# Sum of reciprocals over rows of 1024: another list of loads and operations for the last 24 rows

## Chip, cores and metric

One core of a Trainium2 chip. The metric is the device time of one execution in microseconds (us). An execution has a span, from its first to its last recorded instruction, which lies some 2 us under the device time. "Row" below is one of the 128 slices of 128 partitions by 1024 columns into which the input is cut, numbered 0 to 127; the last 24 are rows 104 to 127.

## The reference

```python
def reference(x):          # x: 32 x 512 x 1024, float32, positive
    return np.sum(1.0 / x, axis=-1).astype(np.float32)
```

## The kernel before

64 MiB are streamed through a ring of 40 rows in SBUF. A row of 1024 values is taken as two halves a and b of 512, by 1/a + 1/b = (a + b) / (a b). So a row needs the product a b, its Ln, an Exp of minus that (exp(-ln y) is 1/y), and a multiply-and-sum on VectorE, against a + b if TensorE has made that in PSUM (a reduction of 512 columns), or else against the row itself (1024 columns). The last 24 rows are written as a list of steps, and the list alone decides in which order each engine meets them.

```python
LAST = 104
LAST_LOADS = [2] * 10 + [1] * 4              # rows in each load
ORDER = """ P104+ P106 L104+ S109 P107 ... E127 T126 T127 """
# c is the row, "+" takes rows c and c+1 in one instruction
# P  product on GpSimd, both halves from SBUF        -> pr (SBUF)
# D  the same product on VectorE, both from SBUF     -> pr
# B  TensorE copies half b into PSUM; V: product on VectorE, a from SBUF, b from PSUM -> pr
# S  TensorE makes a + b in PSUM
# L  Ln of pr on ScalarE;   E  Exp of minus that
# T  reduction on VectorE: 512 columns where the row has an S, else 1024
# W, X  Ln, then Exp of the whole row (1024) on ScalarE, which also sums it (accum_out)
...
        elif kind == "W":
            keep(nc.scalar.activation(out=rows, in_=rows, func=Ln))
        elif kind == "X":
            keep(nc.scalar.activation(out=rows, in_=rows, func=Exp, scale=-1.0,
                                      accum_out=sums[:, c : c + 1]))
...
nc.sync.dma_start(out=out_v, in_=sums)       # one store, after the last sum
```

## Time and profile before

| | before |
|---|---|
| device time, median of the first 3 runs (range) | 169.75 us (169.62 to 170.16) |
| span of the profiled run | 167.9 us |
| last load complete on all 16 engines | 161.46 us |
| ScalarE's last Exp ends / VectorE's last sum is written | 164.62 / 165.45 us |
| from the last load to the last sum | 3.99 us |
| store issued | 165.47 us |

The last four times come from the trace: the landing marks of the input queue and the ends of the last records. The fifth line tells how much lies behind the stream. The lines that carry this reading stand in the prediction. Columns: start, duration, engine, line, operation, output and input.

### The profile page before, as it was taken

The page shows a single profiled execution, that of the slowest core. Times are in us where ns is not written, and L with a number is a line of the kernel's source. Part 1 is how long each engine was busy: PE and PEld are TensorE (multiplying, and loading weights), DVE is VectorE, ACT ScalarE, POOL GpSimd, SP SyncE. Part 2 cuts the span into 40 slices and gives each one's busy share as a digit, 9 for nine tenths or more (in the row PEclk, how much of TensorE's full clock was granted, in tenths as well). Part 3 has the DMA queues.
Part 4 walks back from the last instruction along what each step waited for, and adds up shares of the span by engine and source line. Part 5 has one row for each costly group of instructions (what it writes and reads, how often), then busy time and mean ns, then how long its engine had stood idle before and what let it go on. Part 6 is the DMA issues. An engine that isn't in the chain of part 4 may idle for free.

```text
span 167.9 us, 1307 instructions
## 1 busy us (share of the span) xinstructions
PE 130.8 (78%) x278; PEld 50.5 (30%) x278; DVE 122.8 (73%) x268; ACT 134.1 (80%) x143; POOL 137.7 (82%) x73
## 2 busy tenths in 40 slices
PE   0007999786989869776797869877999988799991
PEld 0003333232323323222332323333343324243340
DVE  0000677768977677885777787778989898999894
ACT  3001898979888897959879787999999998999992
POOL 1007999699996999859996998999999999979780
PEclk9999999999999999999999999999999999999999
DMA  6999999999999999999999999999999999999900
GB/s 195 429 437 429 445 429 437 437 429 429 406 455 414 445 422 449 422 431 437 429 429 429 429 398 429 427 433 433 420 429 408 423 418 424 422 422 414 382 26 18
DMA packets 4471, 67.25 MB, mean 401 GB/s; under 512 B 496, under 2 KB 624, under 8 KB 1136
## 3 DMA queue, kind: packets, MB, share of 16 engines
q1 hardware_dynamic: 4464, 67.18, 94.4%
q8 instruction: 2, 0.03, 0.1%
q14 instruction: 5, 0.04, 0.1%
HBM read 67.11 MB, written 0.07 MB: 400 GB/s over the span
## 4 chain that ended last, share of the span: by engine, by line
DMA 71%; ACT 11%; POOL 10%; DVE 3%; issue 2%; PE 2%; DVEq 0%; SPq 0%; POOLq 0%; ACTq 0%
DMA ring<-in_x_dram 71%; POOL pr L159 8%; ACT pr L231 5%; ACT pr L237 3%; ACT r L237 2%; POOL pr L213 1%; DVE pr L110 1%; PE s L100 1%; DVE ring L110 1%; ACT pr L170 1%; ACT r L175 1%; PE bb L100 1%; DVE pr L222 0%; DVE sums L110 0%; DVEq L287 0%
## 5 line engine op out<-in xcount | busy, mean ns | idle before, releaser
L100 PE MATMUL s<-ring,ident 128*128 128x512 f32 x256 | 121.4, 613 | 32.2 <-DMA ring<-in_x_dram 16.2
L159 POOL TENSOR_TENSOR pr<-ring 128x1024 f32<-128x1024 f32 (+1 forms) x52 | 112.7, 2202 | 21.5 <-DMA ring<-in_x_dram 21.5
L100 PEld LDWEIGHTS s<-ring,ident 128*128 128x128 f32 x256 | 46.9, 193 | 104.1 <-issue 63.3
L170 ACT ACTIVATE pr<-pr 128x1024 f32<-128x1024 f32 x52 | 54.8, 1053 | 26.9 <-POOL pr L159 26.9
L110 DVE CUSTOM_DVE_ANT_1 pr<-ring,r 128x1024 f32<-128x1024 f32 x27 | 33.0, 1221 | 41.4 <-ACT r L175 41.4
L110 DVE CUSTOM_DVE_ANT_1 ring<-ring,r 128x1024 f32<-128x1024 f32 x37 | 44.8, 1217 | 0.2 <-issue 0.2
L110 DVE CUSTOM_DVE_ANT_0 pr<-pr,s 128x512 f32<-128x512 f32 x64 | 41.5, 683 | 0.3 <-ACT pr L237 0.3
L180 ACT ACTIVATE pr<-pr 128x1024 f32<-128x1024 f32 x26 | 27.5, 1057 | 0.8
L175 ACT ACTIVATE r<-pr 128x1024 f32<-128x1024 f32 x26 | 26.7, 1028 | 0.8
L213 POOL TENSOR_TENSOR pr<-ring 128x512 f32<-128x512 f32 (+1 forms) x15 | 24.5, 1648 | 3.0 <-DMA ring<-in_x_dram 2.4
L231 ACT ACTIVATE pr<-pr 128x512 f32<-128x512 f32 (+1 forms) x17 | 13.0, 794 | 1.0 <-DVE pr L222 0.7
L110 DVE DVE_READ_ACCUMULATOR2_ANT sums<- 128x1 f32 x128 | 10.6, 83 | 0.0
L100 PE MATMUL b<-ring,ident 128*128 128x512 f32 x16 | 8.7, 625 | 0.1
L237 ACT ACTIVATE pr<-pr 128x512 f32<-128x512 f32 (+1 forms) x10 | 6.9, 704 | 0.1
L237 ACT ACTIVATE r<-pr 128x512 f32<-128x512 f32 (+1 forms) x11 | 6.8, 625 | 0.1
L148 DVE TENSOR_TENSOR pr<-ring,b 128x512 f32<-128x512 f32 x8 | 5.5, 682 | 0.0
L100 PEld LDWEIGHTS b<-ring,ident 128*128 128x128 f32 x16 | 2.6, 188 | 5.6 <-DMA ring<-in_x_dram 4.1
L100 PE MATMUL bb<-ring,ident 128*128 128x512 f32 x6 | 3.2, 622 | 1.3 <-DMA ring<-in_x_dram 1.2
L222 DVE TENSOR_TENSOR pr<-ring,bb 128x512 f32<-128x512 f32 x3 | 2.1, 686 | 0.7 <-PE bb L100 0.6
L100 PEld LDWEIGHTS bb<-ring,ident 128*128 128x128 f32 x6 | 1.0, 188 | 3.4 <-DVE sums L110 2.0
L71 ACT ACT_TABLE_LOAD x1 | 1.3, 1283 | 0.7 <-PEq L276 0.7
L215 DVE TENSOR_TENSOR pr<-ring 128x512 f32<-128x512 f32 x1 | 0.9, 864 | 0.0
(6 smaller groups left out, 0.9 us busy)
## 6 DMA issues: line engine op xcount, KB each, us to landing
ring<-in_x_dram SPq DMA_DIRECT2D x10, 4096.0 KB, 37.8
ring<-in_x_dram SPq DMA_DIRECT2D x6, 2048.0 KB, 37.0
ring<-in_x_dram SPq DMA_DIRECT2D x10, 1024.0 KB, 26.0
ring<-in_x_dram SPq DMA_DIRECT2D x4, 512.0 KB, 16.8
out_dram<-sums SPq DMA_DIRECT2D x1, 64.0 KB, 1.5
```

Source lines behind the costliest of these rows:

```text
L71: nc.scalar.add_instruction(mybir.InstLoadActFuncSet(name=nc.get_next_instruction_name(), act_func_set_id=act_sets.index("natural_log_exp_ ...
L100: i = nc.tensor.matmul(bank, lhsT=ident, rhs=half, start=k == 0, stop=k == len(halves) - 1,)
L110: i = nc.vector.tensor_tensor_reduce(out=row if out is None else out, in0=row, in1=fac, scale=S, scalar=0.0, op0=mult, op1=plus, accum_out ...
L148: i = nc.vector.tensor_tensor(out=pr[:, j, :], in0=xt[:, q + j, :H], in1=b, op=mult)
L159: i = nc.gpsimd.tensor_tensor(out=pr[:, v:, :], in0=xc[:, v:, :H], in1=xc[:, v:, H:], op=mult)
L170: keep(nc.scalar.activation(out=pr, in_=pr, func=Ln, scale=S))
L175: nc.scalar.activation(out=r, in_=pr[:, e:, :], func=Exp, scale=-1.0)
L180: keep(nc.scalar.activation(out=r, in_=r, func=Exp, scale=-1.0))
L213: keep(nc.gpsimd.tensor_tensor(out=pr, in0=a, in1=b, op=mult))
L222: nc.vector.tensor_tensor(out=pr[:, 0, :], in0=a[:, 0, :], in1=bs[c], op=mult)
L231: keep(nc.scalar.activation(out=pr, in_=pr, func=Ln, scale=S))
L237: keep(nc.scalar.activation(out=r, in_=pr, func=Exp, scale=-1.0))
```

## The change

The intent: get rows in smaller portions at the end of the stream, reorder the work of the last rows, and take row 127 off three engines by doing it whole on ScalarE, so that less is left after the last load.

```diff
-    LAST_LOADS = [2] * 10 + [1] * 4
+    LAST_LOADS = [2] * 1 + [4] * 1 + [2] * 5 + [1] * 8
     ORDER = """
-        P104+ P106 L104+ S109 P107 E104 E105 T104 P108 B109 L106 L107 S107
-        V109 E106 P110+ T105 L108+ E107 S110 T106 E109 P112+ E108 T107 L110+
-        T108 E110 B114 T109 P115 E111 T110 L112+ S114 V114 E112 T111 L114+
-        P116+ S115 T112 E113 E114+ T113 S117 L116 P118+ T114 L117 T115 E116
-        S118 E117 T116 L118+ P120 T117 S119 E118+ D121 L120+ T118 B123 P122
-        T119 E120+ S122 V123 P124 L122 T120 L123 P125 L124 S124 T121 E122 E123
-        P126 T122 E124 S126 T123 L125 P127 L126 T124 E125 S127 E126 T125 L127
-        E127 T126 T127
+        P104 P105 L104+ P107 B106 E104+ V106 P109 B108 L106+ T104 P110+ S108
+        E106+ V108 T105 L108+ S109 T106 L110+ P112+ T107 E108+ S112 E110 T108
+        L112+ P114+ T109 S113 T110 E111 E112+ T111 L114+ P116 S116 T113 E114+
+        T112 P117 L116 T114 P119 B118 L117 E116 S118 V118 E117 P120 T115 L118+
+        P121 S119 T116 E118+ T117 P122 L120+ S122 T118 E120+ D123 L122+ T120
+        S123 P124 E122+ T119 D125 S125 L124 T122 L125 P126 T121 E124 S126 E125
+        T123 L126 T124 W127 E126 T125 X127 T126
     """
```

## The prediction

> **What bounds the kernel now.** The page came first, to see whether the loads or the arithmetic carry the span. These lines are its transfer rows and its chain by engine.
>
> ```profile
> DMA  6999999999999999999999999999999999999900
> GB/s 195 429 437 429 445 429 437 437 429 429 406 455 414 445 422 449 422 431 437 429 429 429 429 398 429 427 433 433 420 429 408 423 418 424 422 422 414 382 26 18
> ...
> DMA 71%; ACT 11%; POOL 10%; DVE 3%; issue 2%; PE 2%; DVEq 0%; SPq 0%; POOLq 0%; ACTq 0%
> ```
>
> The transfers are full through 38 of 40 slices (4.2 us each) at about 425 GB/s; 67.11 MB at that rate are 158 us of a span of 167.9. No other list for the last 24 rows shortens that. It can touch only what lies after the last landing, so I read the end by the microsecond: rates first (columns: stretch, length, busy PE, PEld, DVE, ACT, POOL, clock, DMA share, GB/s).
>
> ```profile
> 158.00:159.00 1.00, 1.00 (x4) 0.42 (x3) 1.00 (x2) 1.00 (x3) 1.00 (x1) 1.00 0.99 393
> 159.00:160.00 1.00, 1.00 (x4) 0.38 (x3) 1.00 (x3) 1.00 (x3) 1.00 (x2) 1.00 0.41 164
> 160.00:161.00 1.00, 1.00 (x4) 0.52 (x3) 1.00 (x3) 1.00 (x3) 1.00 (x2) 1.00 0.16 66
> 161.00:162.00 1.00, 1.00 (x4) 0.43 (x3) 1.00 (x3) 1.00 (x3) 1.00 (x2) 1.00 0.00 0
> ```
>
> The stream thins out at 159.4 and is empty at 161. The landing marks of the input queue in the trace give the same: the last pairs complete at 148.96, 151.45, 153.93 and 156.42, the four single rows at 157.70, 158.98, 160.21 and 161.46. That is 1.245 us a row, singles and pairs alike. But all four engines are at 1.00 in these stretches: they are behind, not waiting for the last row. The timelines show who ends.
>
> ```profile
> 161.26 1.13 ACT L231 ACTIVATE pr<-pr 128x512 f32<-128x512 f32 x2
> 162.31 0.58 ACT L237 ACTIVATE r<-pr 128x512 f32<-128x512 f32 x1
> 162.82 0.61 ACT L237 ACTIVATE pr<-pr 128x512 f32<-128x512 f32 x1
> 163.35 0.61 ACT L231 ACTIVATE pr<-pr 128x512 f32<-128x512 f32 x1
> 163.99 0.63 ACT L237 ACTIVATE pr<-pr 128x512 f32<-128x512 f32 x1
> ```
>
> ```profile
> 156.55 6.33 POOL L213 TENSOR_TENSOR pr<-ring 128x512 f32<-128x512 f32 x5 [1.21 <-DMA ring<-in_x_dram]
> ```
>
> ```profile
> 163.00 1.22 DVE L110 CUSTOM_DVE_ANT_1 ring<-ring,r 128x1024 f32<-128x1024 f32 x1
> 164.15 0.08 DVE L110 DVE_READ_ACCUMULATOR2_ANT sums<- 128x1 f32 x1
> 164.15 0.68 DVE L110 CUSTOM_DVE_ANT_0 pr<-pr,s 128x512 f32<-128x512 f32 x1
> 164.76 0.08 DVE L110 DVE_READ_ACCUMULATOR2_ANT sums<- 128x1 f32 x1
> 164.76 0.68 DVE L110 CUSTOM_DVE_ANT_0 pr<-pr,s 128x512 f32<-128x512 f32 x1
> 165.37 0.08 DVE L110 DVE_READ_ACCUMULATOR2_ANT sums<- 128x1 f32 x1
> ```
>
> Row 127 lands at 161.46. GpSimd starts its product at 161.6 (fifth of a run from 156.55, 1.27 us each, no gap), ScalarE has it as Ln and Exp until 164.6, VectorE's last reduction runs from 164.76, and the accumulator is read at 165.45. From the last landing to there are 4.0 us; the store and the closing barriers take 2.4 us more (165.47 to 167.9), and the device time is 1.84 us over the span (169.74 against 167.9).
>
> **What the Trainium skill says.** "ScalarE: Activation LUTs", section "What ACT_TABLE_LOAD costs", gives an ACTIVATE with immediate operands as 186 ns + 0.833 N ns, with back-to-back ones overlapping by about 93 ns: 1.04 and 0.61 us for N = 1024 and 512, less 0.09. The trace agrees: 1.04 and 0.61, start to start 0.96 and 0.52. So one pair costs 0.96 where two singles cost 1.04; pairing is cheap, not free of delay. "VectorE: DVE Perf Modes", section "The TRN2 errata — SBUF-src ops pay a fixed extra latency per instruction", has fp32 tensor_tensor at N = 512 exactly at 691 ns. The products with one operand in PSUM take 683 ns here, but the one product with both in SBUF took 864; I use 864 for the added one. "DMA: Bandwidth & Descriptors", section "Measured (HBM→SBUF, 128 partitions, SWDGE, issued from GpSimd)", asks for transfers of 1 MiB or more. The single rows are 0.5 MiB and still land every 1.25 us, since others are queued behind them; I take no penalty. For the accumulator output of ScalarE the same VectorE page, section "Two Vector instructions with no wait between them", says that on VectorE it is a second instruction (83 ns in the trace); no page gives ScalarE's time. I call 0.1 to 0.25 us my estimate, from those 83 ns.
>
> **The change, part by part.** Counting the built programs' instructions that serve rows 104 to 127, at start-to-start times from the timelines:
> - ScalarE before: 10 of 1024 and 28 of 512 columns, 10 x 0.96 + 28 x 0.52 = 24.2 us. After: 19 and 12, so 18.2 + 6.2 = 24.4 us, plus one accumulator output. The words "Lns of single rows" mislead: single Lns fall from 10 to 5.
> - GpSimd before: 5 pairs at 2.37 and 10 singles at 1.275, 24.6 us; after 3 and 12, 22.4 us.
> - VectorE before: 12 long reductions at 1.145, 12 short at 0.605, 3 products from PSUM at 0.605, one from SBUF at about 0.80: 23.6 us. After: 12, 11, 3 and 2: 23.8 us.
> - TensorE before: 12 row sums at 1.72 and 3 copies at 0.86, 23.2 us; after 11 and 3, 21.5 us.
>
> So work leaves the two engines that do not end the kernel, and none leaves ScalarE and VectorE, which do. The gain can only come from the shape of the last microseconds: row 127 no longer passes through GpSimd, TensorE and VectorE, but is one Ln and one accumulating Exp of 1024.
>
> Up to row 103 each queue is unchanged, so I laid out each queue after that by hand: an instruction starts when its engine is free (times above) and 0.035 us after the last thing that it waits for; an ACTIVATE that reads the one directly before costs 0.12 more. The same laying out of the kernel before puts its last reduction at 164.62, where the trace has 164.76: the method is 0.14 early on VectorE and 0.07 on ScalarE. For the changed kernel: the load of four rows lands complete only at 139.0 (rows 106 and 107 were there at 136.4), which holds GpSimd 0.9 us and is made good by 149.0, when rows 116 and 117 land. From there GpSimd runs singles to 156.7, then waits for row 124 (157.70) and row 126 (160.21); its last product ends at 161.52.
>
> ScalarE from 157.59, without a gap over 0.12: Ln of 122-123 (1.08), their Exp (0.96), Ln 124 with a wait on VectorE's product of 125 (0.63), Ln 125, Exp 124, Exp 125, Ln 126 (4 x 0.52), Ln of all of row 127 (0.96, starting at 162.35), Exp 126 (0.52), accumulating Exp of 127 from 163.83 for 1.05: 164.88, and with the 0.07 and the accumulator 165.05 to 165.2.
>
> VectorE from 157.61, also without a gap: rows 120, 119, product 125, rows 122, 121, 123, 124, 125, 126 = 3 x 1.145 + 4 x 0.605 + 0.80 + 0.75 = 7.4 us: 165.0, with the 0.14 165.15.
>
> Row 127 is there 0.9 us before ScalarE comes to it: the last landing is not on the path. Both ends fall near 165.15 instead of 165.45, so about 0.3 us come off; the store and the closing barriers follow as before. 169.75 - 0.3 = 169.45, put down as 169.4.
>
> **The rivals.**
> (a) The tail is bound by the last landing, and the new way for the last row gives all that it promises: Ln at 161.5, Exp to 163.6, about 1.7 us off, 168.0. For it: the diff's intent, and DMA is 71% of the chain. Against it: four engines at 1.00 after 159, and Ln 126 standing before Ln 127 in ScalarE's queue.
> (b) Eight loads of 0.5 MiB in place of four drain more slowly: 396 to 410 GB/s were seen in some stretches from 154 on, where 418 to 426 were usual. At 4% of 1.25 us that is 0.05 us a row, 0.2 us for four more single rows; as the landing has 0.9 us to spare, the end moves by less than that. Only over 1 us of delay would eat the gain: 169.8 to 170.3. A starved queue speaks against itself: row 127's load may be issued when rows 118-119 land (151.45, eight loads before it), 10 us ahead of its own landing.
> (c) The accumulator output is long (0.5 us or more) or the in-place passes over the ring cost more than 1.05: ScalarE ends the kernel at 165.5 or later, 169.8.
> (d) A miss in the middle: the four-row load or two more dependent Ln-Exp pairs leave VectorE 0.3 us more behind: 169.7.
>
> **Range and chances.** 2% are 3.4 us, and all of the time from the last landing to the last sum is 4.0, of which row 127 alone needs 2.1 in any case. Faster by 2% is out of reach; slower by 2% would need a broken stream. The runs of before spread from 169.62 to 170.16, wider than the effect; so I take 168.9 to 170.0 about 169.4, with 0.98 for within 2%.
>
> **What would show it.** Right: landings of the last row within 0.2 us of 161.46; ScalarE and VectorE at 1.00 from 158 to 164; Ln of row 127 at about 162.4, its idle before it none; both engines ending within 0.3 us of each other near 165.1; the store at 165.2. Wrong: ScalarE idle before row 127 with the input as releaser (then rival a or b), an accumulator read over 0.4 us (c), or gaps on VectorE between 150 and 158 over 1 us (d). The prediction falls if the last sum ends before 164.5 or after 165.8.

## More of the kernel before

One pair is added here, since it turned out to matter: a product on VectorE (first fence, row 121) that runs beside one on GpSimd (second fence, row 120).

```profile
155.02 0.86 DVE L215 TENSOR_TENSOR pr<-ring 128x512 f32<-128x512 f32 x1
```

```profile
154.06 1.28 POOL L213 TENSOR_TENSOR pr<-ring 128x512 f32<-128x512 f32 x1
```

GpSimd's ends at 155.34. VectorE's begins before that, and ends 0.55 us after it.

## The result, and the profile after

169.38 us, median of 6 runs (169.16 to 169.86), against 169.78 (169.62 to 170.16). The ratio is 0.9976, 95% interval 0.9958 to 0.9995: some 0.4 us (0.1 to 0.7), clear of zero and well within 2%. A ratio here is the mean time of one kernel's fast runs over the mean of the other's in the same rounds, so not quite the ratio of the medians. The profiled run of the changed kernel (169.71 us) was one of the longer of its six: its stream is about 0.4 us later throughout than that of the kernel before, and its last load completes at 161.82.

The spans of all six runs tell a little more than the times. They average 167.37 us, and the device time is 2.08 us longer than they are; the kernel before, in the eleven runs recorded beside e1 to e4, has 167.93 us and 1.90 us. These are not the same rounds. But they say that the span fell by some 0.56 us and that 0.2 us of this did not reach the device time. Runs e5, e6, e10 and e11 also have 2.1 us outside the span, the others 1.8 to 1.9; what makes the difference is not known.

The page after, its transfer rows and its chain by engine:

```profile
DMA  6999999999999999999999999999999999999910
GB/s 203 422 446 430 446 422 399 461 399 446 414 409 454 407 446 422 442 424 446 430 430 422 414 418 434 424 434 434 420 426 413 436 416 416 422 413 410 409 71 18
...
DMA 72%; POOL 11%; ACT 9%; DVE 2%; issue 2%; PE 1%; ACTq 1%; SPq 0%; POOLq 0%
```

Little has changed here: the last slice but one moves 71 GB/s where it was 26, as this stream ended later. The rates by the microsecond (columns as in the prediction):

```profile
159.00:160.00 1.00, 0.87 (x3) 0.15 (x2) 1.00 (x5) 1.00 (x2) 0.53 (x1) 1.00 0.71 283
160.00:161.00 1.00, 1.00 (x3) 0.52 (x4) 1.00 (x4) 1.00 (x3) 0.26 (x1) 1.00 0.21 86
161.00:162.00 1.00, 1.00 (x3) 0.39 (x3) 1.00 (x2) 1.00 (x3) 1.00 (x1) 1.00 0.05 20
162.00:163.00 1.00, 1.00 (x4) 0.38 (x2) 1.00 (x5) 1.00 (x3) 0.02 (x1) 1.00 0.00 0
163.00:164.00 1.00, 0.55 (x2) 0.00 (x0) 1.00 (x3) 1.00 (x2) 0.00 (x0) 1.00 0.00 0
```

GpSimd now has room from 159 on (0.53, 0.26, 1.00, 0.02); TensorE has none until its last record ends at 163.55 (164.45 before). VectorE and ScalarE are still at 1.00 to the end. The end of ScalarE's timeline, then GpSimd's, then VectorE's:

```profile
161.49 0.61 ACT L236 ACTIVATE pr<-pr 128x512 f32<-128x512 f32 x1
162.05 0.63 ACT L230 ACTIVATE pr<-pr 128x512 f32<-128x512 f32 x1
162.59 1.04 ACT L248 ACTIVATE ring<-ring 128x1024 f32<-128x1024 f32 x1
163.53 0.61 ACT L236 ACTIVATE pr<-pr 128x512 f32<-128x512 f32 x1
164.05 1.04 ACT L251 ACTIVATE ring<-ring 128x1024 f32<-128x1024 f32 x1
165.00 0.19 ACT L251 ACTIVATION_READ_ACCUMULATOR ring<-ring 128x1 f32 x1
```

```profile
139.42 17.53 POOL L212 TENSOR_TENSOR pr<-ring 128x512 f32<-128x512 f32 x11 [1.07 <-DMA ring<-in_x_dram]
158.25 1.28 POOL L212 TENSOR_TENSOR pr<-ring 128x512 f32<-128x512 f32 x1 [1.30 <-DMA ring<-in_x_dram]
160.74 1.28 POOL L212 TENSOR_TENSOR pr<-ring 128x512 f32<-128x512 f32 x1 [1.21 <-DMA ring<-in_x_dram]
```

```profile
157.00 0.69 DVE L214 TENSOR_TENSOR pr<-ring 128x512 f32<-128x512 f32 x1
...
159.72 0.69 DVE L214 TENSOR_TENSOR pr<-ring 128x512 f32<-128x512 f32 x1
...
164.43 0.68 DVE L109 CUSTOM_DVE_ANT_0 pr<-pr,s 128x512 f32<-128x512 f32 x1
165.03 0.08 DVE L109 DVE_READ_ACCUMULATOR2_ANT sums<- 128x1 f32 x1
```

ScalarE ends at 165.19 and VectorE at 165.12: the two end together, as they were meant to. From the last load to the last sum are 3.36 us, 0.63 less than before. And VectorE's two products from SBUF fall exactly into GpSimd's two gaps: 157.00 to 157.69 in the gap from 156.95 to 158.25, 159.72 to 160.41 in that from 159.53 to 160.74.

### The profile page after: what moved, and what is told of

It reads as the page before. It is cut to its first block, busy times and chain, and to the rows that moved or that the text cites. A ratio compares the mean times of both kernels' runs of the same rounds, so it can differ in the third digit from the quotient of the medians.

```text
span 167.6 us, 1286 instructions
## 1 busy us (share of the span) xinstructions
PE 130.3 (78%) x274; PEld 50.2 (30%) x274; DVE 122.6 (73%) x267; ACT 134.8 (80%) x137; POOL 135.7 (81%) x73
## 4 chain that ended last, share of the span: by engine, by line
DMA 72%; POOL 11%; ACT 9%; DVE 2%; issue 2%; PE 1%; ACTq 1%; SPq 0%; POOLq 0%
DMA ring<-in_x_dram 72%; POOL pr L158 11%; ACT pr L230 3%; ACT pr L169 2%; ACT pr L236 2%; DVE ring L109 1%; ACT r L236 1%; PE bb L99 1%; ACT r L174 1%; ACT ring L248 1%; ACTq L286 1%; DVE pr L109 0%; DVE pr L221 0%; SPq L139 0%; ACT pr L179 0%
## 5 line engine op out<-in xcount | busy, mean ns | idle before, releaser
L99 PEld LDWEIGHTS s<-ring,ident 128*128 128x128 f32 x252 | 46.3, 193 | 101.8 <-issue 61.9
L109 DVE CUSTOM_DVE_ANT_1 pr<-ring,r 128x1024 f32<-128x1024 f32 x30 | 36.6, 1221 | 41.5 <-ACT r L174 40.8
L109 DVE CUSTOM_DVE_ANT_1 ring<-ring,r 128x1024 f32<-128x1024 f32 x34 | 41.3, 1217 | 0.0
L109 DVE CUSTOM_DVE_ANT_0 pr<-pr,s 128x512 f32<-128x512 f32 x63 | 40.9, 683 | 0.0
L212 POOL TENSOR_TENSOR pr<-ring 128x512 f32<-128x512 f32 (+1 forms) x15 | 22.3, 1504 | 3.9 <-DMA ring<-in_x_dram 3.6
L230 ACT ACTIVATE pr<-pr 128x1024 f32<-128x1024 f32 (+1 forms) x14 | 12.5, 900 | 0.5 <-DVE pr L221 0.5
L236 ACT ACTIVATE r<-pr 128x1024 f32<-128x1024 f32 (+1 forms) x8 | 6.4, 806 | 0.1
L236 ACT ACTIVATE pr<-pr 128x1024 f32<-128x1024 f32 (+1 forms) x7 | 6.0, 863 | 0.1
```

The source lines that it names most:

```text
L99: i = nc.tensor.matmul(bank, lhsT=ident, rhs=half, start=k == 0, stop=k == len(halves) - 1,)
L109: i = nc.vector.tensor_tensor_reduce(out=row if out is None else out, in0=row, in1=fac, scale=S, scalar=0.0, op0=mult, op1=plus, accum_out ...
L212: keep(nc.gpsimd.tensor_tensor(out=pr, in0=a, in1=b, op=mult))
L230: keep(nc.scalar.activation(out=pr, in_=pr, func=Ln, scale=S))
L236: keep(nc.scalar.activation(out=r, in_=pr, func=Exp, scale=-1.0))
```

## The experiments

The theory was that of the prediction: the backlog of ScalarE and VectorE sets the end, and only what shortens or balances these two queues moves it. Rival A: the last load's landing sets it. Rival B: small loads drain more slowly, and that moves the end. All results are correct unless said, and all runs are fast but the single one of e12, whose state is unknown; times are medians, and "behind" is the time from the last load to the last sum in the trace (3.99 before, 3.36 after).

| run | time, us | before, same rounds | ratio (95% interval) | last load | behind |
|---|---|---|---|---|---|
| changed kernel | 169.38 | 169.78 | 0.9976 (0.9958 to 0.9995) | 161.82 | 3.36 |
| e1 old loads | 171.25 | 169.78 | 1.0085 (1.0071 to 1.0100) | 161.33 | 5.47 |
| e2 old list | 170.11 | 169.78 | 1.0017 (1.0001 to 1.0033) | 161.43 | 4.41 |
| e3 last row back | 170.04 | 169.78 | 1.0014 (0.9999 to 1.0029) | 161.58 | 4.28 |
| e4 last row alone | 170.06 | 169.78 | 1.0015 (1.0001 to 1.0030) | 161.34 | 4.34 |
| e5 pairs 120 | 172.11 | 170.50 | 1.0113 (1.0083 to 1.0143) | 162.15 | 5.44 |
| e6 no four | 170.26 | 170.50 | 1.0010 (0.9978 to 1.0043) | 161.46 | 3.38 |
| e7 product GpSimd | 170.63 | 170.50 | 1.0028 (1.0000 to 1.0056) | 161.75 | 4.44 |
| e8 two rows ScalarE | 170.80 | 170.50 | 1.0043 (1.0008 to 1.0078) | 161.90 | 4.25 |
| e9 less to load (wrong result) | 169.22 | 169.85 | 0.9966 (0.9947 to 0.9986) | 159.04 | 6.23 |
| e10 less, before (wrong result) | 169.96 | 169.85 | 1.0006 (0.9992 to 1.0021) | 158.95 | 6.38 |
| e11 products busy | 170.12 | 169.85 | 1.0018 (1.0001 to 1.0034) | 161.50 | 4.09 |
| e12 = e2, one look | 170.05 | 169.85 | one run | 161.38 | 4.40 |

Runs e5 to e8 fell on a restless chip (before: 169.65 to 172.75 there, one of the eleven runs slow and left out of the ratios); for them "behind" is the better figure. Their times all lie above the figures expected (e7 by 0.03 us, the others by 0.3 to 0.8), as that of the kernel before lies above its 169.78 elsewhere.

### e1: the new list with all the old loads

```diff
-    LAST_LOADS = [2] * 1 + [4] * 1 + [2] * 5 + [1] * 8
+    LAST_LOADS = [2] * 10 + [1] * 4
```

> The new list of operations, but the old loads (ten pairs, four singles). My theory (the end is set by the backlog of ScalarE and VectorE, and the new list is fitted to finer loads): row 120 now comes as a pair with 121 at about 153.9, so the product of 120 waits, ScalarE is idle some 1.2 us before the Ln of rows 120-121, and all after it moves: laid out by hand from the times of the kernel before, last sum at about 166.0 instead of 165.15, so 170.2 to 170.4 us, slower than before by 0.3 to 0.4%. Rival A (the last landing sets the end, the last row on ScalarE is what gains): loads do not matter as long as the last four are singles, 169.4. Rival B (single loads drain more slowly and the new list gains more than it shows): last landing 0.2 to 0.4 us earlier than in the changed kernel, time 169.1 to 169.3.

171.25: the direction of my theory, but 0.9 us more than its figure; rivals A and B are off by more. ScalarE's wait before the Ln of rows 120-121 is there as foreseen (1.02 us, third fence); a second wait, of 0.89 us, was not. VectorE's products, then GpSimd's, then ScalarE's waits in this run:

```profile
156.66 1.64 DVE L215 TENSOR_TENSOR pr<-ring 128x512 f32<-128x512 f32 x1
...
160.50 1.57 DVE L215 TENSOR_TENSOR pr<-ring 128x512 f32<-128x512 f32 x1
```

```profile
153.96 5.46 POOL L213 TENSOR_TENSOR pr<-ring 128x512 f32<-128x512 f32 x4 [1.18 <-DMA ring<-in_x_dram]
160.25 1.27 POOL L213 TENSOR_TENSOR pr<-ring 128x512 f32<-128x512 f32 x1 [0.83 <-DMA ring<-in_x_dram]
```

```profile
156.51 1.06 ACT L231 ACTIVATE pr<-pr 128x1024 f32<-128x1024 f32 x1 [1.02 <-POOL pr L213]
...
162.11 0.63 ACT L231 ACTIVATE pr<-pr 128x512 f32<-128x512 f32 x1 [0.89 <-DVE pr L215]
```

The same product that takes 0.69 us in a gap of GpSimd takes 1.64 and 1.57 beside a GpSimd product. GpSimd's four take 5.46 where four of 1.28 would be 5.12: it waits too. The Trainium skill has this: "SBUF — State Buffer", section "Who interferes with whom", says that a VectorE instruction with two SBUF inputs contends with a GpSimd instruction that reads SBUF, and that the one that has the shared port pair keeps the other out. The trace agrees, as the table shows. I had not applied it. Individual records of all runs give it numbers (differences taken before rounding):

| run, row | VectorE's product | GpSimd's product under way ended | VectorE's end after that |
|---|---|---|---|
| before, 121 | 155.02 to 155.89 | 155.34 | 0.55 |
| e1, 123 | 156.66 to 158.29 | 157.74 | 0.55 |
| e1, 125 | 160.50 to 162.07 | 161.53 | 0.55 |
| e4, 121 | 154.90 to 155.75 | 155.21 | 0.55 |
| e5, 123 | 157.45 to 159.07 | 158.51 | 0.55 |
| e5, 125 | 161.30 to 162.87 | 162.32 | 0.55 |
| e7, 123 | 157.05 to 158.67 | 158.12 | 0.55 |
| e10, 121 | 154.11 to 155.87 | 155.33 | 0.55 |
| e11, 106, 118, 123 | 139.94 to 140.90, 153.02 to 153.77, 157.19 to 157.93 | 140.35, 153.22, 157.38 | 0.55 each |

So VectorE's 0.69 us begin, by these ends, when GpSimd's product has 0.14 us left, whenever VectorE's record starts. Where VectorE's starts within those last 0.14 us (e2, e12, and row 108 in e11), it takes its 0.68 to 0.69. The other way about, a GpSimd product of one row whose record begins inside VectorE's ends 1.13 to 1.15 us after it, instead of 1.28 us after its own start (157.78 to 159.42 in e1; also in e2, e5, e7, e10, e11 and e12; the exception, row 124 in e11, begins in the last 0.03 us and takes 1.28). A product of VectorE with one input in PSUM is not held: that of row 108 in the changed kernel takes 0.69 us (142.37 to 143.06) in the middle of a GpSimd product (141.90 to 144.28).

### e2 and e12: the old list with the new loads

```diff
     LAST_LOADS = [2] * 1 + [4] * 1 + [2] * 5 + [1] * 8
-    ORDER = new list
+    ORDER = old list
```

> The old list of operations with the new loads (2, 4, five of 2, eight of 1). My theory: rows come earlier than the old list asks for them, nothing on ScalarE or VectorE moves; laid out by hand the last sum falls within 0.05 us of before: 169.7 to 169.85, ratio 1.000. Rival A: the same, 169.75 (the last row lands at the same time and takes the old path). Rival B (small loads drain more slowly): last landing 0.3 us later or more, and as the product of row 127 starts 0.15 us after its landing in the kernel before, the time rises to 169.9 to 170.2.

170.11, against 169.7 to 169.85 expected. The last load is where it was (161.43), so rival B's reason is not the cause, though its figure fits. What differs is one gap in VectorE's queue, before the reduction of row 125: the wait for the Exp of that row ends at 162.94 in the trace, and the reduction starts at 163.39. In the kernel before it starts 0.11 us after that Exp.

> The second run of this series again (old list, new loads), for one look: it was 0.33 us slower than before, where I had expected nothing, and its profile showed VectorE starting the reduction of row 125 0.48 us after the Exp that it waits for, 0.11 in the kernel before. If the gap belongs to the program, it is there again, at the same instruction, between 0.4 and 0.5 us; if it was chance, it is gone and the end is 165.4 to 165.6 at a landing of 161.4.

```profile
162.22 0.68 DVE L110 CUSTOM_DVE_ANT_0 pr<-pr,s 128x512 f32<-128x512 f32 x1
162.83 0.09 DVE L110 DVE_READ_ACCUMULATOR2_ANT sums<- 128x1 f32 x1
163.34 1.22 DVE L110 CUSTOM_DVE_ANT_1 ring<-ring,r 128x1024 f32<-128x1024 f32 x1 [0.42 <-POOL pr L213]
```

It is there again, 0.49 us after the Exp (162.27 plus 0.58), so it belongs to this program. The view names GpSimd as releaser, but the GpSimd product of row 125, the only one whose row this reduction touches, had ended at 160.34. What holds VectorE for 0.4 us there stays open. What is settled is that the new loads alone, with the old list, gain nothing.

### e3: row 127 the old way in the new list

```diff
-  ... P126 T121 E124 S126 E125 T123 L126 T124 W127 E126 T125 X127 T126
+  ... P126 T121 E124 S126 E125 T123 P127 L126 T124 S127 E126 T125 L127 E127 T126 T127
```

> The changed kernel with row 127 the old way: product on GpSimd, sum on TensorE, Ln and Exp of 512, reduction on VectorE last. My theory: ScalarE is done 1 us sooner (Exp of 127 ends at about 164.1), but VectorE gets one reduction more (0.6 us) and its last one starts at about 164.95 plus: last sum at 165.65 to 165.8, 169.9 to 170.0, so the row on ScalarE is worth about 0.5 us in this list. Rival A (only the landing counts): what the last row saves, 4.0 minus 2.1 us at most, is lost whole, 170.5 to 171. Rival C (the order of the other rows carries the gain, the last row none): 169.4, as the changed kernel.

170.04. ScalarE ends at 164.32, VectorE at 165.87, just over my figure (165.65 to 165.8), since its last reduction waited 0.30 us for TensorE's sum of row 127. Rivals A and C are out. In this list the last row on ScalarE is worth 4.28 minus 3.36 = 0.9 us of "behind" and 0.66 us of the medians. The mean spans, 168.28 and 167.37, agree with the 0.9.

### e4: row 127 alone, in the kernel before

```diff
-  ... T123 L125 P127 L126 T124 E125 S127 E126 T125 L127 E127 T126 T127
+  ... T123 L125 W127 L126 T124 E125 E126 T125 X127 T126
```

> The kernel before, old loads and old list, with row 127 alone changed: its whole Ln where the product stood (after the Ln of 125), its accumulating Exp last. My theory: the whole Ln takes 0.96 us of a ScalarE that has no gap, and VectorE waits 1.0 us for the Exp of row 125 behind it; last sum at 165.7 to 165.8, 170.0 to 170.2, slower than before by 0.2%. Rival A (the last row's own path sets the end): about as fast as the changed kernel or faster, 168.5 to 169.4, with ScalarE's Ln of 127 directly at the landing (161.5).

170.06; VectorE ends at 165.68 and had waited 0.95 us for the Exp of row 125, behind the whole Ln that starts at 161.67, 0.33 us after the landing. Rival A expected this to be as good as the whole change; it is slower than the kernel before. The row on ScalarE pays only in a list that has made room for it.

### e5: rows 120 to 123 as pairs again

```diff
-    LAST_LOADS = [2] * 1 + [4] * 1 + [2] * 5 + [1] * 8
+    LAST_LOADS = [2] * 1 + [4] * 1 + [2] * 7 + [1] * 4
```

> The changed kernel, but rows 120 to 123 loaded as two pairs again (2, 4, seven of 2, four of 1). Theory now (after the run with all the old loads came out at 171.25, 0.9 us over my figure, with VectorE's products of rows 123 and 125 at 1.64 and 1.57 us beside a GpSimd product against 0.69 in the changed kernel): the two engines exclude each other on products read from SBUF, and the single loads leave GpSimd idle just when VectorE does its own. So this alone should bring back all of it: both products over 1.4 us, ScalarE waiting about 1 us before the Ln of rows 120-121 and 0.9 us before that of 125, 171.1 to 171.4. Rival: the 1.4 us come from other parts of the old load list (pairs 106-109 earlier, last landing), then 169.4 to 170.

Behind: 5.44 us, as in e1 (5.47), with products of 1.62 and 1.57 us and waits of ScalarE of 1.03 and 0.89. So all of e1's loss hangs on four rows that come singly or in pairs. Singly, GpSimd takes rows 120 to 122 as they land and is through with 122 (156.95) before row 124 lands (158.09): there is a gap for VectorE's product of 123. In pairs it starts row 120 some 1.3 us later (154.76 against 153.10, in a stream 0.33 us later), and works without a break over the time of that product.

### e6: no load of four rows

```diff
-    LAST_LOADS = [2] * 1 + [4] * 1 + [2] * 5 + [1] * 8
+    LAST_LOADS = [2] * 8 + [1] * 8
```

> The changed kernel with rows 104 to 119 all in pairs (eight of 2, eight of 1; no load of four rows). Theory: the load of four rows costs GpSimd 0.9 to 1.1 us at 138 to 139 and this is made good by row 116; the end does not move, 169.3 to 169.5. Rival D of the prediction (the load of four leaves the engines behind): 168.8 to 169.1.

Behind: 3.38 us, as the changed kernel. The time is no evidence (ratio 1.0010, interval 0.9978 to 1.0043, on the restless chip). By this one profile the load of four is neither gain nor loss at the end. This run also shows the changed list at the landing of the kernel before: last load at 161.46, last sum at 164.84.

### e7: product of row 125 moved to GpSimd, with the old loads

```diff
     LAST_LOADS = [2] * 10 + [1] * 4
-  ... E122+ T119 D125 S125 L124 ...
+  ... E122+ T119 P125 S125 L124 ...
```

> The new list with all the old loads, as in the first run of this series (171.25), but the product of row 125 on GpSimd in place of VectorE. Theory of exclusion: one of the two long waits of VectorE is gone (1.57 us, of which 0.9 were waiting) and its own 0.6 too; the Ln of 125 waits less; laid out by hand with the exclusion the last sum is at about 166.0 instead of 166.8, so 170.3 to 170.6; VectorE's product of 123 still 1.6 us. Rival (GpSimd is the scarce engine there, another product on it delays row 126): 171.2 or more.

Last sum at 166.19, 170.63: one of e1's two collisions is gone and 1.03 us of "behind" with it (5.47 to 4.44), although GpSimd has more to do. The other collision is still there (1.62 us for row 123).

### e8: row 126 whole on ScalarE as well

```diff
-  ... P126 T121 E124 S126 E125 T123 L126 T124 W127 E126 T125 X127 T126
+  ... T121 E124 E125 T123 W126 T124 W127 X126 T125 X127
```

> The changed kernel with row 126 too done whole on ScalarE (Ln and accumulating Exp of 1024, each), nothing of it left on GpSimd, TensorE and VectorE. Theory (ScalarE's backlog sets the end): it gets 0.96 + 1.14 for 0.52 + 0.52, so 1.05 us more, VectorE ends 0.6 us sooner; last sum at about 166.1, 170.3 to 170.5. Rival A (only the way of the last rows after their landing counts): 169.4 or less.

ScalarE ends at 166.15, VectorE at 164.58; the ratio is 1.0043. Doubling what helped once costs 0.9 us of "behind": ScalarE is the one that ends, with VectorE 1.6 us ahead of it. The balance of the two is the gain, not the way of the row.

### e9 and e10: two rows less to load

Wrong results: rows 104 and 105 are not loaded, and the ring's old content is used in their place.

```diff
-    c0 = LAST
+    c0 = LAST + 2      # and LAST_LOADS without its first pair
     for n in LAST_LOADS:
```

> Wrong on purpose: the changed kernel without the load of rows 104 and 105 (the ring still holds rows 64 and 65 there), all else the same, so that every later row lands 2.5 us earlier, the last near 159.0. Theory (the engines' backlog sets the end, and in the changed kernel the landing of row 126 is only some 0.1 to 0.2 us from setting it): laid out by hand the last sum comes 0.16 us earlier than in the changed kernel, against a landing 2.5 us earlier: end minus landing 5.5 to 5.9 us instead of 3.4, ScalarE without a gap over 0.5 us from 150, 169.1 to 169.4. Rival A (the last landing sets the end): end minus landing stays 3.4, 166.9 to 167.2.

> Wrong on purpose: the kernel before without the load of rows 104 and 105, so that every later row lands 2.5 us earlier. Theory: last sum 0.13 us earlier by hand, 169.5 to 169.8, end minus landing 6.2 to 6.5 us. Rival A: 167.2 to 167.5.

The last load completes 2.8 us earlier than in the changed kernel's profile (159.04 against 161.82) and 2.5 us earlier than in that of the kernel before (158.95 against 161.46), and the ends stay: 165.27 against 165.19, and 165.33 against 165.45. "Behind" grows to 6.23 and 6.38. Rival A, which wanted 167, is out for both kernels. But e10 says less than its end suggests. There the earlier rows let ScalarE run ahead, by 1.32 us at the Ln of rows 118-119 (152.69 against 154.01). Then VectorE's product of row 121 met one of GpSimd, took 1.76 us, and kept ScalarE waiting for 1.15 us; so the end should have come earlier without this collision, and its fit to my 0.13 us is in part luck. VectorE's product and ScalarE's wait in e10:

```profile
154.11 1.76 DVE L215 TENSOR_TENSOR pr<-ring 128x512 f32<-128x512 f32 x1
```

```profile
155.97 1.06 ACT L231 ACTIVATE pr<-pr 128x1024 f32<-128x1024 f32 x1 [1.15 <-DVE pr L215]
```

In e9 no product of VectorE from SBUF was held (0.69 us each), so e9 is the one that carries the argument. For e9 my figure for "behind" (5.5 to 5.9) was too low: ScalarE had one gap of 0.76 us from 153 on, waiting for VectorE's product of row 118, that I had not laid out. The end of ScalarE's timeline in e9:

```profile
162.15 0.61 ACT L231 ACTIVATE pr<-pr 128x512 f32<-128x512 f32 x1
162.67 1.04 ACT L249 ACTIVATE ring<-ring 128x1024 f32<-128x1024 f32 x1
163.62 0.61 ACT L237 ACTIVATE pr<-pr 128x512 f32<-128x512 f32 x1
164.14 1.04 ACT L252 ACTIVATE ring<-ring 128x1024 f32<-128x1024 f32 x1
165.08 0.18 ACT L252 ACTIVATION_READ_ACCUMULATOR ring<-ring 128x1 f32 x1
```

Row 127 has been there since 159.04, and its Ln starts at 162.67, as late as in the changed kernel.

### e11: three more products from SBUF where GpSimd is at work

```diff
-  ... B106 E104+ V106 ... B108 ... V108 ... B118 ... V118 ...
+  ... D106 E104+      ...      ... D108 ...      ... D118 ...
```

> The changed kernel with the products of rows 106, 108 and 118 on VectorE straight from SBUF, in place of TensorE's copy into PSUM and a product from there; GpSimd is at work without a break at these times. Theory of exclusion: VectorE's product starts when the GpSimd product under way has 0.15 us left, and GpSimd's next waits in turn; by hand 0.8, 0.7 and 1.5 us for the three (0.69 undisturbed), GpSimd's product beside row 108's longer by 0.4, last sum at 166.3 instead of 165.15: 170.6 to 171.0. Rival (SBUF products are slow on VectorE only where rows have just landed): all three at 0.69, 169.2 to 169.5, or a little faster, as TensorE has less to do.

0.95, 0.68 and 0.74 us, last sum at 165.59, 170.12. The mechanism holds (the 0.55 us in the table, and GpSimd's eleven products take 18.30 us instead of 17.53), the rival falls. The size was off: row 118's product met only the last 0.2 us of a GpSimd product, not most of one, so the end is 0.7 us early on my figure. What a collision costs depends on a few tenths of a microsecond of alignment. That is why it cannot be read from a list.

Of the runs with a right result none has less "behind" than the changed kernel.

## Why the prediction was right, point by point

- **The time.** 169.4 stated, 169.38 measured; the worked-out gain of 0.3 us (169.45 before rounding) against about 0.4. The closeness is partly luck, as two errors meet in it. At the same landing the last sum comes 0.6 us earlier than before (e6 against the kernel before), twice the gain laid out; and 0.2 us of that is lost outside the span, where the prediction let all follow as before. The middle of the argument, that work leaves the engines that do not end the kernel and that the gain is in the last microseconds alone, is what e3, e4 and e8 show: undo the last row's way, do it alone, or do it twice, and the kernel is slower each time, by about what the queues of ScalarE and VectorE say.
- **The end of both queues.** "Both ends fall near 165.15" came out as 165.19 and 165.12. But this fit is partly luck: the profiled run's stream was 0.36 us later than the 161.46 that I had put in (so one of the signs listed, a last landing within 0.2 us of that, failed). At a landing of 161.46, e6 has the same list end at 164.84, so the laying out was about 0.3 us pessimistic. Two terms of the sum were mis-sized. The product of row 125 stood at 0.80 from start to start and took 0.60 (159.72 to 160.32). And the 0.14 that I added to VectorE, from the kernel before, belonged to that kernel: from 157.96 on VectorE took 7.16 us in the changed one, where my terms sum to 7.4 with the product at 0.80 and to 7.2 with it at 0.60.
- **The skill and the product.** I set aside the 691 ns of the Trainium skill ("VectorE: DVE Perf Modes", section "The TRN2 errata — SBUF-src ops pay a fixed extra latency per instruction") for a product with both inputs in SBUF, as one took 864 here. That was wrong: the page's figure holds (0.69 in a gap of GpSimd), and the 864 held a wait for GpSimd. I was misled by a mean of one sample, and by reading a duration as work.
- **The last landing is not on the path.** Right for row 127 (landed at 161.82, its Ln at 162.59) and shown by e9. "The landing has 0.9 us to spare" was still too wide: row 126 lands at 160.60, its product ends at 162.02 and its Ln starts at 162.05, while ScalarE was free at 162.01. In this list the landing of row 126 and the backlog bind at the same moment. A later landing should move the end at once, which no run tests; an earlier one gains nothing, as e9 shows.
- **Rival B.** Right to reject: with eight single rows the last load completes between 161.38 and 161.90 (seven profiles), with four between 161.33 and 162.15 (five). But its effect is there, and small: counted from the landing of row 119, eight single rows take 10.12 to 10.17 us in these profiles, two pairs and four singles 9.99 to 10.02. So the "1.245 us a row, singles and pairs alike" is 1.24 in pairs and 1.26 to 1.27 singly; the four more singles cost 0.12 us, within the 0.2 allowed.
- **Rival C.** The accumulator read is a second record of 0.19 us. It begins 0.95 us after its Exp does and ends 0.09 after it (165.09 against 165.19 in rounded figures), just under the 0.1 to 0.25 estimated.
- **The loads.** I took them to be of little account: true with the old list, not with the new one. E5 shows that the new list would be 2.1 us slower in "behind" without rows 120 to 123 as singles, by GpSimd's gaps. The prediction got past this without seeing it: it laid out GpSimd's gaps, and VectorE's products happened to fall into them.

## What to carry to other kernels

Behind a saturated stream, lay out the queues of the engines that end last, instruction by instruction. A faster path for the last item gained here only where the engine that takes it had room (e3 and e4), and where two engines end together, moving a row from one to the other did not help (e8). Before giving VectorE a product with both inputs in SBUF, look whether GpSimd is reading SBUF at that moment; if it is, VectorE waits for it, and smaller loads can open the gap that it needs. A duration that varies for one shape (here 0.69, 0.86, 1.57, 1.64) may be work plus a wait; here the shortest one was the work.

## What the Trainium skill lacked or had wrong

- "SBUF — State Buffer", section "Who interferes with whom", is right that a two-SBUF-input VectorE instruction and a GpSimd product exclude each other, but gives no times for it. In eleven collisions here VectorE's 512-column fp32 product ends 0.55 us after the GpSimd product does (0.69 undisturbed), so VectorE goes on when GpSimd's record has 0.14 us left; a GpSimd product of one row behind VectorE's ends 1.13 to 1.15 us after it (1.28 undisturbed).
- "ScalarE: Activation LUTs" has no time for the accumulator output. Here it is a second record of 0.19 us that ends 0.09 us after its 1024-column Exp.
- "DMA: Bandwidth & Descriptors", section "Measured (HBM→SBUF, 128 partitions, SWDGE, issued from GpSimd)", advises 1 MiB or more for each transfer. Loads of 0.5 MiB, issued 10 us and more before their landing, landed every 1.21 to 1.30 us, 1.27 on average for eight of them, which is 414 GB/s and 2% slower for each row than those of 1 MiB (2.48 to 2.49 us for two rows).
- No page has the 0.4 us for which VectorE stood still in e2 and e12 after all that it waited for was done.
